# A one-core transformer kernel: unused tiles move its on-chip operands to multiples of 512 bytes

## The chip, the core and the metric

The kernel runs on one core of one Trainium2 chip. Its time is the device time of one execution in microseconds (us), and a kernel is judged by the median of several executions. A separate execution is recorded by the hardware profiler, and every stretch, row and duration below that is not called a median comes from that one recording. Engine names are those of the profile: PE multiplies matrices (PEld is its loading of the operand that stays in the array), DVE and ACT are the vector and the scalar engine, POOL is the general engine, SP issues most transfers (DMA).

## What is computed

Two layers of a diffusion backbone work on 256 latent tokens of width 2048, in float32. Cut to what matters here:

```python
def reference(x, c, ctx, c_ctx, ada_w, ...):
    x_lat, x_ctx = x, ctx
    for l in range(2):
        sh1, sc1, g1, sh2, sc2, g2 = split(silu(c) @ ada_w[l] + ada_b[l], 6)
        h = modulate(x_lat, norm_mix[l], sh1, sc1)
        if l == 0:
            hc = modulate(x_ctx, ...)               # 256 context tokens
            y = even_mixer(h, hc, ...)              # h @ ev_w_in, gated delta rule || attention, @ ev_w_out
        else:
            y = shortconv_mixer(h, ...)             # h @ od_w_in, 3-tap convolution, @ od_w_out
        x_lat = x_lat + g1 * y
        h2 = modulate(x_lat, norm_ffn[l], sh2, sc2)
        x_lat = x_lat + g2 * ((silu(h2 @ w_gate[l]) * (h2 @ w_up[l])) @ w_down[l])
    return rmsnorm(x_lat, final_norm)
```

`ada_w[l]` is 2048 x 12288, `w_gate` and `w_up` are 2048 x 5632, `w_down` is 5632 x 2048. Nearly all bytes and nearly all arithmetic are the weights times a few hundred tokens.

## The kernel before

**Every large product is split into three.** A float32 operand is written as a rounded part (hi) and a remainder (lo), both in the type `float32r`, and a product is hi x hi + hi x lo + lo x hi, three matmuls that add into one PSUM bank. Weights arrive in pieces of 128 rows x 1024 columns (512 KB, tile `raw`). `split_w` (from L236) makes `whi` on ACT (L173) and `wlo` on DVE (L244) from each. The activations are split once per stage, into `hlhi`/`hllo` and `hchi`/`hclo` (normed latent and context tokens of layer 0, L584), `yhi`/`ylo` (the first mixer's output), `fhi`/`flo` (FFN input), `dhi`/`dlo` and `zhi`/`zlo` (the second mixer's input and its gated result), and, for the down projection, `ahi`/`alo`, split piece by piece from `prodT` (L176, L177).

**Two kinds of stream use them.** `tm_stream` holds a 128 x 128 block of the activation in the array and sends 512 columns of `whi` or `wlo` past it: L292, L293 and L295 are its three products, L301, L302 and L303 the same for the last two blocks of a sum. A step of it, one weight piece for two blocks of tokens, is 2 x 2 x 3 = 12 such matmuls. A stream of 2048 rows by 1024 columns has 16 steps, so 192 matmuls; the down projection has 44 steps for each 1024 columns. `fm_stream` does the reverse: a 128 x 128 block of `whi` or `wlo` is held and 256 tokens of h are sent past it (L322). Both load the held block anew for every matmul, so each MATMUL has its LDWEIGHTS.

**What runs when.** First the modulation vectors of layer 0 (L555), then `fm_stream` for keys, values and queries with the delta rule's small products in between, then the attention, then `tm_stream` for ev_w_out (with y), layer 0's FFN (11 streams for gate and up, 88 steps for down), the second mixer (6 streams for od_w_in with d, 2 for od_w_out with z), and layer 1's FFN. Beside these streams the other columns of `ada_w` are read as `araw` and summed on DVE (L376, L411).

**Where tiles lie.** Each tile takes the same byte range in all 128 partitions. Pools are filled from the left or, where `side="right"` is given, from the right end of the on-chip memory, one tile after the other; a pool opened later begins where the earlier one ends. Tiles through the class `Rows` are rounded up to 16 floats, so they begin at multiples of 64 bytes, and nothing in the kernel asks for more. A tile's start therefore depends on the sizes of all tiles before it on its side: `edge` and the tiles of `epool`, `gw` (pool "gdn"), `rpool`, the FFN's `ap_` and the second mixer's `dp` are such predecessors, and the diff touches these.

The order of instructions on each engine comes from the recording layer, which is given the program in the order in which `body` writes it.

Of the kernel before, what the change touches and what calls it, by code (L numbers as in the profile page):

```python
# [23 lines left out]
F32 = mybir.dt.float32  # L24
# [85 lines left out]
def body(tc, x, c, ctx, c_ctx, ada_w, ada_b, norm_mix, norm_ffn, ffn_w_gate, ffn_w_up, ffn_w_down,  # L110
# [27 lines left out]
    def pool(name, bufs=1, stack=root, **kw):  # L138
        if kw.get("space") is not bass.MemoryType.DRAM:
            kw.setdefault("reuse_waits", "tile")  # L140
        p = stack.enter_context(tc.tile_pool(name=name, bufs=bufs, **kw))
        return p if "space" in kw else Rows(p)

    cpool = pool("const")
    edge = pool("edge", side="right").p.tile([128, 8], F32, name="edge")
    epool = pool("even")
    wstk = Stack()
    wp = dict(pool=pool("weights", stack=wstk), raw=RAW, split=3)
# [9 lines left out]
    def smt():  # L158
        small.append(small.pop(0))
        return small[0].tile([128, 512], F32, name="sm", tag="sm")  # L160
# [11 lines left out]
    def acopy(dst, src):  # L172
        ACT.activation(dst, src, AF.Copy)  # L173
# [16 lines left out]
    def transpose(dst, src):  # L190
        n = src.shape[0]
        return PE.transpose(dst, src, ident[:n, :n])  # L192
# [245 lines left out]
    def load_row(l, seg):  # L438
        r = rpool.tile([128, D], F32, name="row", tag="row", bufs=1)
        src = row_d[l, seg]  # L440
        ACT.dma_start(r, bass.AP(tensor=src.tensor, offset=src.offset, ap=[[0, 128], [1, D]]))
        return r
# [36 lines left out]
    def drive(stream, pump=None, n=1, every=1, counts=False):  # L479
        for i, _ in enumerate(stream):  # L480
            steps[0] += counts
            while counts and plan and plan[0][0] <= steps[0]:
                plan.pop(0)[1]()
            if later and i % every == every - 1:
                f, args = later.pop(0)
                f(*args)
            if pump:
                pump(n)
# [262 lines left out]
    gw = pool("gdn", stack=rstk, side="right")  # L751
# [38 lines left out]
    eg = epool.tile([128, 3, 2, 4, 8], F32, name="eg")  # L790
    negegc = epool.tile(gsh, F32, name="negegc")
    brest = epool.tile(gsh, F32, name="brest")

    def gates():
        w = abp
# [370 lines left out]
    lga.close()  # L1166
    yp = pool("y", stack=lgs, side="right")

    yhi, ylo = [], []
    for g in range(3):  # L1170
        for l_, n_, tag in ((yhi, "yhi", "diag"), (ylo, "ylo", "lsol")):
# [85 lines left out]

    rpool = pool("resid")
    xs = rpool.tile([128, 2, D], F32, name="xs")
    ssx = rpool.tile([128, 2, 4], F32, name="ssx")  # L1260
    ss2 = rpool.tile([128, 2], F32, name="ss2")
    jk = rpool.tile([128, 512], F32, name="jk")
# [23 lines left out]
    def norm_h(hi, lo, sc_, sh_):  # L1286


        ns = Stack()
        pool_ = pool("norm", stack=ns)  # L1290
        r = [None, None]
        for n in range(4):
            ks_ = slice(n * 4, n * 4 + 4)
            for t in range(2):
                if not n:
                    r[t] = norm_row(t)
                xt_ = pool_.tile([128, 512], F32, name="xc", tag="xc", bufs=4)
                xi = DVE.tensor_scalar(xt_, xs[:, t, n * 512:(n + 1) * 512], r[t], None, op0=OP.mult)
                p = smt()
                for j in range(4):  # L1300
                    transpose(p[:, j * 128:(j + 1) * 128], xt_[:, j * 128:(j + 1) * 128])
                m = pool_.tile([128, 4, 128], F32, name="modt", tag="modt", bufs=2)
                tok = slice(t * 128, t * 128 + 128)
                for j in range(4):
                    k = n * 4 + j
                    q = p[:, j * 128:(j + 1) * 128]
                    mi = ACT.activation(hi[:, k, tok], q, AF.Identity, bias=sh_[:, k:k + 1], scale=sc_[:, k:k + 1])
                    DVE.tensor_scalar(m[:, j, :], q, sc_[:, k:k + 1], sh_[:, k:k + 1], op0=OP.mult, op1=OP.add)
                DVE.tensor_tensor(lo[:, ks_, tok], m, hi[:, ks_, tok], op=OP.subtract)  # L1309
                if not n:  # L1310
                    behind = (mi if not t else behind[0], xi)
        ns.close()
        return behind

    def split_on_the_fly(pool_, src):
        def f(k):
            hi = pool_.tile([128, 256], F32R, name="ahi", tag="ahi", bufs=3)
            lo = pool_.tile([128, 256], F32R, name="alo", tag="alo", bufs=3)
            s = src(k)
            if len(s.shape) == 3:  # L1320
                split(hi.rearrange("p (t e) -> p t e", t=2), lo.rearrange("p (t e) -> p t e", t=2), s)
            else:
                split(hi, lo, s)
            return lambda t: hi[:, t * 128:(t + 1) * 128], lambda t: lo[:, t * 128:(t + 1) * 128]
        return f
# [32 lines left out]
    def ffn(l, jobs_fn, n_jobs):  # L1358
        fs = Stack()
        hp = pool(f"ffn_h{l}", stack=fs)  # L1360
        hi = hp.tile([128, KT, 256], F32R, name="fhi", tag="fhi", bufs=1)
        lo = hp.tile([128, KT, 256], F32R, name="flo")
        normed = norm_h(hi, lo, scc[l, 3], shc[l, 3])
        ap_ = pool(f"ffn_a{l}", stack=fs)
        jobs = jobs_fn(ap_)
        pump = Pump(jobs, PS[l], n_jobs)
        pp = pool(f"ffn_p{l}", stack=fs)
        prodT = pp.tile([128, FK, 256], F32, name="prodT")

        def lhs(k):  # L1370
            return lambda t: hi[:, k, t * 128:(t + 1) * 128], lambda t: lo[:, k, t * 128:(t + 1) * 128]

        def finish(prod, w, c0):

            for f in range(0, w // 128, 2):
                p = smt()
                for kk in range(2):
                    for t in range(2):
                        transpose(p[:, kk * 256 + t * 128:kk * 256 + (t + 1) * 128],
                                  prod[:, t, (f + kk) * 128:(f + kk + 1) * 128])  # L1380
                acopy(prodT[:, c0 // 128 + f:c0 // 128 + f + 2, :], p.rearrange("p (k t) -> p k t", k=2))

        for c0 in range(0, 5120, 1024):
            sg = pp.tile([128, 2, 1024], F32, name="sg", tag="sg", bufs=1)

            def ge(ti, n, p):
                ACT.activation(sg[:, ti, n * 512:(n + 1) * 512], p, AF.Silu)

            def ue(ti, n, p):
                v = sg[:, ti, n * 512:(n + 1) * 512]  # L1390
                DVE.tensor_tensor(v, p, v, op=OP.mult)

            drive(tm_stream([(ffn_w_gate[l], c0, 1024)], ks, lhs, [0, 1], ge, None if c0 else normed), pump)
            drive(tm_stream([(ffn_w_up[l], c0, 1024)], ks, lhs, [0, 1], ue), pump)
            finish(sg, 1024, c0)
        sg = pp.tile([128, 2, 1024], F32, name="sg", tag="sg", bufs=1)

        def le(ti, n, p):
            v = sg[:, ti, 0:512]
            if n == 0:  # L1400
                ACT.activation(v, p, AF.Silu)
            else:
                DVE.tensor_tensor(v, p, v, op=OP.mult)

        drive(tm_stream([(ffn_w_gate[l], 5120, 512), (ffn_w_up[l], 5120, 512)], ks, lhs, [0, 1], le), pump)
        finish(sg, 512, 5120)
        otf = split_on_the_fly(pp, lambda k: prodT[:, k, :])
        row = load_row(l, 5)
        fn = None
        if l:  # L1410
            fn = hp.tile([128, D], F32, name="fn", tag="fhi", bufs=1)
            ACT.dma_start(fn, bass.AP(tensor=final_norm.tensor, offset=final_norm.offset, ap=[[0, 128], [1, D]]))
        for half in range(2):
            drive(tm_stream([(ffn_w_down[l], half * 1024, 1024)], list(range(FK)), otf, [0, 1],
                            resid_evac(row, half * 1024, fn)), pump)
        pump.finish()
        fs.close()

    ffn(0, lambda ap_: [ada_job(ap_, 0, 5, "row"), ada_job(ap_, 1, 0, "sh"), ada_job(ap_, 1, 1, "sc", gamma=g_mix[1]), ada_job(ap_, 1, 3, "sh"), ada_close()], 132)


    ds = Stack()
    dp = pool("od", stack=ds)
# [1 line left out]
    dlo = dp.tile([128, KT, 256], F32R, name="dlo")  # L1425
    zhi = dp.tile([128, KT, 256], F32R, name="zhi")
    zlo = dp.tile([128, KT, 256], F32R, name="zlo")
    up = [dp.tile([128, 258], F32, name=f"upad{i}") for i in range(2)]
    normed = norm_h(dhi, dlo, scc[1, 0], shc[1, 0])
    adp = pool("od_a", stack=ds)  # L1430
    pump = Pump([ada_job(adp, 1, 2, "row"), ada_job(adp, 1, 4, "sc", gamma=g_ffn[1]), ada_close()], PO, 68)
# [48 lines left out]
    ds.close()  # L1480

    ffn(1, lambda ap_: [ada_job(ap_, 1, 5, "row"), ada_close()], 36)


# [39 lines left out]
```

## Time and profile before

| | |
|---|---|
| median of 3 executions | 2813.17 us (2809.87 to 2813.56) |
| span of the profiled execution | 2817.0 us |
| its share of the full TensorE clock | 0.986 |
| bytes moved | 677.62 MB, 241 GB/s on average |

The record holds no time of the profiled execution other than its span, from the first to the last instruction; it is 3.8 us above the median. The busy time of PE in the profile counts an interval in which any matmul is in flight. Neighbouring matmuls overlap: one of 512 columns takes some 0.39 us from its start to its end, but the next one starts about 0.23 us after it. So PE's real rate is read from the distance between starts, not from the mean duration of a matmul, and a busy share near 100% does not say that the matmuls could not follow one another faster.

### The profile page before, as it was taken

To read this page: it belongs to the slowest core of one execution; us is meant where nothing else is said; L and a number is where in the kernel's file an instruction comes from. 1 tells how busy PE (TensorE), PEld (TensorE's weight loads), DVE (VectorE), ACT (ScalarE), POOL (GpSimd) and SP (SyncE) were. 2 spreads that over 40 slices of the span, in tenths; PEclk is the share of its full clock that TensorE was granted. 3 is DMA by queue.
4 is the path that set the end of the run, shared out by engine and by line. 5 is a ranking of instruction groups with operands and counts; after the bars stand their busy time and mean duration, and the time that the engine had idled before them with its cause. 6 is when DMAs were issued, how large, how long until landed. Compare 5 with 4: busy or idle time off the path is not lost.

```text
span 2817.0 us, 39969 instructions
## 1 busy us (share of the span) xinstructions
PE 2712.2 (96%) x14935; PEld 2260.4 (80%) x14935; DVE 1931.3 (69%) x2653; ACT 1290.4 (46%) x1923; POOL 48.0 (2%) x77
## 2 busy tenths in 40 slices
PE   6999999999989999999999999999999999999998
PEld 3798989887768788888888878787878888888886
DVE  2377877875768888887676667897688644445565
ACT  3267543323454644444455555344454444445554
POOL 0000000000000000000000000000000000000000
PEclk9999999998999999999999999999999999999999
DMA  9944587886658699999775557998659766666563
GB/s 340 328 136 154 150 269 240 289 253 198 194 182 278 215 336 331 347 333 325 271 270 189 189 158 276 325 321 289 197 199 332 239 191 187 187 201 202 189 190 123
DMA packets 284990, 677.62 MB, mean 241 GB/s; under 512 B 57081, under 2 KB 100705, under 8 KB 283387
## 3 DMA queue, kind: packets, MB, share of 16 engines
q1 hardware_dynamic: 280420, 665.59, 71.2%
q10 hardware_dynamic: 4375, 9.48, 0.9%
q8 instruction: 117, 1.92, 0.3%
q14 instruction: 78, 0.64, 0.1%
HBM read 655.54 MB, written 19.43 MB: 240 GB/s over the span
## 4 chain that ended last, share of the span: by engine, by line
PE 67%; DMA 16%; DVE 9%; issue 4%; ACT 3%; SPq 1%; POOL 0%; DVEq 0%; ACTq 0%
PE mm L292 15%; PE mm L293 15%; PE mm L295 15%; DMA araw<-in_ada_w_dram 11%; PE mm L322 9%; DVE acc L376 4%; DVE wlo L244 3%; PE sm L192 2%; PE mm L301 1%; PE mm L303 1%; PE mm L302 1%; DMA bq<-in_ev_rpb_dram 1%; PE sm L555 1%; PE gd L322 1%; DMA acc<-in_ada_b_dram 1%
## 5 line engine op out<-in xcount | busy, mean ns | idle before, releaser
L173 ACT ACTIVATE whi<-raw 128x1024 fp32r<-128x1024 f32 x800 | 842.8, 1059 | 872.2 <-PE mm L295 628.4
L244 DVE TENSOR_TENSOR wlo<-raw,whi 128x1024 fp32r<-128x1024 f32 x800 | 970.2, 1222 | 394.1 <-ACT whi L173 387.0
L293 PE MATMUL mm<-wlo,fhi 128*128 128x512 f32 x1232 | 469.9, 392 | 0.2 <-DVE wlo L244 0.2
L292 PE MATMUL mm<-whi,fhi 128*128 128x512 f32 x1232 | 468.6, 396 | 0.0
L295 PE MATMUL mm<-whi,flo 128*128 128x512 f32 x1232 | 393.4, 392 | 0.1
L376 DVE SCALAR_TENSOR_TENSOR acc<-araw,cT,acc 128x1024 f32<-128x1024 f32 x224 | 287.3, 1283 | 143.4 <-DMA araw<-in_ada_w_dram 131.5
L295 PEld LDWEIGHTS mm<-whi,flo 128*128 128x128 f32 x1232 | 231.1, 188 | 51.1 <-DVE flo L1309 0.3
L293 PEld LDWEIGHTS mm<-wlo,fhi 128*128 128x128 f32 x1232 | 231.6, 188 | 49.4 <-DVE wlo L244 0.6
L292 PEld LDWEIGHTS mm<-whi,fhi 128*128 128x128 f32 x1232 | 232.1, 188 | 48.5
L293 PE MATMUL mm<-wlo,ahi 128*128 128x512 f32 x672 | 258.9, 395 | 0.0
L292 PE MATMUL mm<-whi,ahi 128*128 128x512 f32 x672 | 258.0, 396 | 0.0
L295 PE MATMUL mm<-whi,alo 128*128 128x512 f32 x672 | 210.9, 395 | 0.0
L322 PE MATMUL mm<-hllo,whi 128*128 128x256 f32 x608 | 172.3, 288 | 0.0
L176 ACT ACTIVATE ahi<-prodT 128x256 fp32r<-128x256 f32 x176 | 72.9, 417 | 198.2 <-DVE wlo L244 179.6
L322 PE MATMUL mm<-hlhi,whi 128*128 128x256 f32 x570 | 160.9, 291 | 2.3 <-DVE hlhi L583 1.9
L322 PE MATMUL mm<-hlhi,wlo 128*128 128x256 f32 x570 | 157.8, 288 | 0.5 <-DVE wlo L244 0.5
L411 DVE SCALAR_TENSOR_TENSOR acc<-araw,cT,acc 128x512 f32<-128x512 f32 x192 | 142.7, 747 | 15.5 <-DMA araw<-in_ada_w_dram 13.8
L295 PEld LDWEIGHTS mm<-whi,alo 128*128 128x128 f32 x672 | 126.6, 188 | 29.5
L292 PEld LDWEIGHTS mm<-whi,ahi 128*128 128x128 f32 x672 | 126.6, 188 | 29.4
L293 PEld LDWEIGHTS mm<-wlo,ahi 128*128 128x128 f32 x672 | 126.6, 188 | 29.2
L177 DVE TENSOR_TENSOR alo<-prodT,ahi 128x256 fp32r<-128x256 f32 x176 | 74.4, 424 | 83.9 <-PE mm L295 78.6
L293 PE MATMUL mm<-wlo,dhi 128*128 128x512 f32 x336 | 123.9, 395 | 0.6 <-DVE wlo L244 0.6
(418 smaller groups left out, 4182.1 us busy)
## 6 DMA issues: line engine op xcount, KB each, us to landing
araw<-in_ada_w_dram SPq DMA_DIRECT2D x288, 512.0 KB
raw<-in_ffn_w_down_dram SPq DMA_DIRECT2D x176, 512.0 KB
raw<-in_ffn_w_gate_dram SPq DMA_DIRECT2D x160, 512.0 KB
raw<-in_ffn_w_up_dram SPq DMA_DIRECT2D x160, 512.0 KB
raw<-in_ev_w_in_dram SPq DMA_DIRECT2D x112, 512.0 KB
araw<-in_ada_w_dram SPq DMA_DIRECT2D x192, 256.0 KB
raw<-in_od_w_in_dram SPq DMA_DIRECT2D x96, 512.0 KB
raw<-in_ev_w_out_dram SPq DMA_DIRECT2D x32, 512.0 KB
```

Of the source, the lines that this page charges most:

```text
L173: ACT.activation(dst, src, AF.Copy)
L176: ACT.activation(hi, src, AF.Copy)
L177: (eng or DVE).tensor_tensor(lo, src, hi, op=OP.subtract)
L192: return PE.transpose(dst, src, ident[:n, :n])
L244: last_lo[0] = DVE.tensor_tensor(lo, raw, hi, op=OP.subtract).ins
L292: PE.matmul(ps[ti][n], a, hi[:, n * 512:(n + 1) * 512], start=first, stop=False)
L293: PE.matmul(ps[ti][n], a, lo[:, n * 512:(n + 1) * 512], start=False, stop=False)
L295: last_mm[0] = PE.matmul(ps[ti][n], b, hi[:, n * 512:(n + 1) * 512], start=False, stop=False).ins
L301: PE.matmul(ps[ti][n], lh(t), hi[:, c_], start=False, stop=False)
L322: last_mm[0] = PE.matmul(ps[f][:, n * 256:(n + 1) * 256], wt, mv(w, k), start=False, stop=i == len(ks) - 1 and g == len(group) - 1 and j = ...
L376: DVE.scalar_tensor_tensor(acc, raw, cT[:, k:k + 1], acc, op0=OP.mult, op1=OP.add)
L411: DVE.scalar_tensor_tensor(accs[n], raws.pop(i), cT[:, k:k + 1], accs[n], op0=OP.mult, op1=OP.add)
```

## The change

Six pools get a few bytes that nobody reads or writes, or a tile that is larger than needed, so that the tiles behind them begin elsewhere:

```diff
-    edge = pool("edge", side="right").p.tile([128, 8], F32, name="edge")
+    edge = pool("edge", side="right").p.tile([128, 120], F32, name="edge")
...
     brest = epool.tile(gsh, F32, name="brest")
+    epool.tile([128, 48], F32, name="pad_e")
...
     yp = pool("y", stack=lgs, side="right")
+    gw.tile([128, 48], F32, name="pad_g")
...
     xs = rpool.tile([128, 2, D], F32, name="xs")
+    rpool.tile([128, 80], F32, name="pad_r")
...
         ap_ = pool(f"ffn_a{l}", stack=fs)
+        ap_.tile([128, 80], F32, name="pad_a")
...
-    up = [dp.tile([128, 258], F32, name=f"upad{i}") for i in range(2)]
+    up = [dp.tile([128, 384], F32, name=f"upad{i}")[:, 0:258] for i in range(2)]
```

No instruction is added, removed or moved. On each of the five engines the built program has the same operations on the same tiles in the same order, with waits on the same semaphores, and the PSUM banks are the same. What differs is where tiles begin. The start of each tile in the built program, as the remainder of its byte address divided by 512:

| tiles | before | now |
|---|---|---|
| `raw`, `whi`, `wlo` (weight pieces, all buffers, all stages) | 320 | 0 |
| `h`, `hlhi`, `hllo`, `hchi`, `hclo` | 320 | 0 |
| `yhi`, `ylo` | 128 | 0 |
| `fhi`, `flo` | 0 | 0 |
| `prodT`, `ahi`, `alo`, `sg` | 192 | 0 |
| `dhi`, `dlo`, `zhi`, `zlo` | 0 | 0 |
| `u_t`, `b_t`, `ocv` | 128 | 0 |
| `acc`, `araw` in layer 0's first mixer | 448 | 0 |
| `acc`, `araw` in the FFN | 0 | 320 |
| `acc`, `araw` in the second mixer | 128 | 0 |
| tiles of the delta rule (`kT`, `ktok`, `gm`, `state`, `xdT` and others) | 128 | 0 |
| `araw0` and `xn` of the start | 128 and 0 | 192 and 64 |

The blocks that a matmul holds are 512 bytes wide in a partition and those that it sends are 1024 or 2048, so each such block has the remainder of its tile.

## The prediction

> **What bounds the kernel now.** I read the page's busy times first, then PE's busy time stage by stage, then the chain of waits inside single stages for the distance between matmul starts.
>
> ```profile
> PE 2712.2 (96%) x14935; PEld 2260.4 (80%) x14935; DVE 1931.3 (69%) x2653; ACT 1290.4 (46%) x1923; POOL 48.0 (2%) x77
> ```
>
> The next view cuts the last two thirds of the span into stages: layer 0's FFN (gate and up, then down), the second mixer (its input product, then its output product), layer 1's FFN.
>
> ```profile
> core 0: us, PE busy (x), PEclk, DMA share, GB/s
> 944.00:1425.00 481.00, 479.67 (x2163) 1.00 0.90 320
> 1425.00:1680.00 255.00, 250.55 (x1102) 0.99 0.61 197
> 1680.00:1955.00 275.00, 270.57 (x1216) 0.99 0.87 300
> 1955.00:2074.00 119.00, 114.26 (x523) 0.97 0.55 177
> 2074.00:2557.00 483.00, 482.28 (x2163) 1.00 0.70 225
> 2557.00:2817.00 260.00, 246.35 (x1065) 0.98 0.54 174
> sum 1873.00, PE 1843.68; mean PE 307.28
> ```
>
> In 1873 us PE is without work for 29. DMA is high in two of the stages and yet PE does not stand still there. So these stages are worth their number of matmuls times the distance between two starts, and that distance is what this change can touch, since no instruction moves.
>
> The distance is not the same everywhere, although the matmuls of lines L292, L293 and L295 are all 512 columns wide. Rows of the chain, in order of time (start, length, what; "x2" are two matmuls): first layer 1's FFN, then its like for the second mixer's output product, the first mixer's output product, layer 0's down projection, and the latent-and-context product with h.
>
> ```profile
> 2310.35 0.46 PE mm L295 x2
> ...
> 2325.46 0.46 PE mm L295 x2
> ```
>
> ```profile
> 2020.87 0.46 PE mm L295 x2
> ...
> 2029.11 0.46 PE mm L295 x2
> ```
>
> ```profile
> 852.93 0.47 PE mm L295 x2
> ...
> 864.13 0.47 PE mm L295 x2
> ```
>
> ```profile
> 1491.03 0.47 PE mm L295 x2
> ...
> 1527.29 0.46 PE mm L295 x2
> ```
>
> ```profile
> 514.88 0.23 PE mm L293
> ...
> 526.67 0.23 PE mm L295
> ```
>
> A pair at L295 returns after six matmuls. FFN: 11 returns, 15.11 us / 66 = **228.9 ns**. z: 6 returns, 8.24 / 36 = **228.9**. y: 8 returns, 11.20 / 48 = **233.3**. Down: 26 returns, 36.26 / 156 = **232.4**. With h: 52 matmuls one by one, 11.79 / 52 = **226.7**. All sent pieces (`whi`, `wlo`) begin at remainder 320 of 512. Only the held operand's remainder differs, and the distance goes with it: 320 gives 226.7; 0 gives 228.9 (fhi, and zhi the same); 192 gives 232.4; 128 gives 233.3. The shortest is where both begin at the same remainder. That dhi, also at 0, has 228.9 as well is taken over from these.
>
> **The change part by part.** It puts held and sent operand of all these products at remainder 0, so equal, as they are today only with h. My theory is that the difference of the two remainders decides, not the remainders: the load of the next block runs beside the matmul, and where the two begin alike it costs least. Then every row above goes to 226.7 ns. The counts, from the loops and checked on two rows of groups:
>
> ```profile
> L292 PE MATMUL mm<-whi,fhi 128*128 128x512 f32 x1232 | 468.6, 396 | 0.0
> L292 PE MATMUL mm<-whi,ahi 128*128 128x512 f32 x672 | 258.0, 396 | 0.0
> ```
>
> Gate and up: 11 streams x 192 x 2 layers = 4224 (a third at L292 and L301 is 1408, of which 14 of 16 steps, 1232, are at L292, as the row says). Down: 88 steps x 12 x 2 = 2112 (704 a third, 42 of 44 steps 672). Second mixer: 6 x 192 = 1152 with d, 2 x 192 = 384 with z. First mixer's output: 2 x 192 = 384 with y. The sum:
>
> - gate and up, 4224 x (228.9 - 226.7) = 9.3 us
> - d and z, 1536 x 2.2 = 3.4 us
> - down, 2112 x (232.4 - 226.7) = 12.0 us
> - y, 384 x (233.3 - 226.7) = 2.5 us
>
> Together **27 us**. Of the 576 wide products with h (384 for the attention's values, 192 for the output gate) nothing changes by this theory: they are at equal remainders before and after. Their 256-wide form at L322 holds a block of the weights and sends h:
>
> ```profile
> 339.93 23.03 PE mm L322 x192
> ```
>
> 23.03 / 192 = 119.9 ns, 320 against 320; I cost it at nothing. Ahead of 944 us only y has a term.
>
> The other engines read and write the same tiles. DVE's sum over `araw` stands at remainder 0 in layer 0's FFN and at 128 in the second mixer; the groups of DVE in 1000 to 1200 us and in 1750 to 1900 us:
>
> ```profile
> L376 DVE SCALAR_TENSOR_TENSOR acc<-araw,cT,acc 128x1024 f32<-128x1024 f32 x55 | 70.6, 1283 | 33.2 <-DMA araw<-in_ada_w_dram 32.2 <-issue 0.3
> L376 DVE SCALAR_TENSOR_TENSOR acc<-araw,cT,acc 128x1024 f32<-128x1024 f32 x39 | 50.0, 1282 | 24.5 <-DMA araw<-in_ada_w_dram 24.3
> ```
>
> 1283 against 1282 ns: DVE does not see the remainder. Nor do the transfers, as far as these rows go: the wait for `araw` is 32.2 / 55 = 0.59 us each at remainder 0 and 24.3 / 39 = 0.62 at 128. So the one place where the change makes a start less round (`araw` and `acc` in the FFN, 0 to 320) I cost at nothing. Were it the whole difference of those two waits, 0.03 us x 160 sums in both FFNs = 5 us of DVE, hidden by PE's own work, since DVE is 69% busy and the splits have spare time; were that cover gone, 5 us. The start's `araw0` and `xn` shift by 64 bytes likewise.
>
> What is late next when PE goes 1 to 2.5% faster in these stages? A step of 12 matmuls falls from 2.75 to 2.72 us.
>
> ```profile
> L244 DVE TENSOR_TENSOR wlo<-raw,whi 128x1024 fp32r<-128x1024 f32 x800 | 970.2, 1222 | 394.1 <-ACT whi L173 387.0
> ```
>
> DVE needs for it 1.22 us of split and at most one sum of 1.28. There is room, and the 90% DMA share of the first FFN stage comes from `araw` pieces that are fetched ahead.
>
> The trace cannot show what a sent piece at remainder 0 costs, since in before all of them start at 320. Bounds: from above, the slowest row, 233.3 ns for everything: 5760 x 4.4 + 2112 x 0.9 + 576 x 6.6 = 31 us lost. From below, the same products while the clock is at half:
>
> ```profile
> 636.00:640.00 4.00, 4.00 (x10) 0.50 0.87 282
> ```
> ```profile
> 636.53 0.43 PE mm L293
> ...
> 639.94 0.43 PE mm L292
> ```
>
> 8 matmuls in 3.41 us are 426 ns, at full clock 213: at half speed nothing is added to the 512 columns. At 213 for everything the gain would be 5760 x 15.9 + 2112 x 19.4 + 384 x 20.3 + 576 x 13.7 = 148 us, and some 3000 at L322 (3 x 768 + 2 x 384 by the loops) x 13 = 39 more. I take 226.7, the nearest row with equal remainders, between those ends.
>
> [...]
>
> **The rivals.**
>
> *A larger gain.* A piece that begins at a round address may by itself be sent faster. For it: blocks of 32 and 64 columns instead of 128 are held at L777 and L778, with the same h at 320 sent past:
>
> ```profile
> 183.50 0.28 PE L780 MATMUL sm<-hllo,abw 128*32 128x256 f32 x1
> ...
> 186.79 0.28 PE L777 MATMUL sm<-hllo,abw 128*32 128x256 f32 x1
> ```
>
> 29 distances in 3.29 us, 113.4 ns against 119.9, so 6.5 ns of the excess over 106.5 (half of 213) belong to the wide load and another 6.9 to something else, perhaps the start at 320. Against it: these 113.4 have the sent operand at 320 too, so the start alone cannot be all of it. If half of the wide load's part went (223.3 instead of 226.7), the gain would be 5760 x 5.6 + 2112 x 9.1 + 384 x 10 + 576 x 3.4 = 57 us, with 3000 x 3.3 = 10 at L322 67: **2746 us**. If all of it went, 220: 106 us, **2707**.
>
> *No difference, or little.* The distance may go with the held operand alone, whatever is sent: then 0 is 228.9 for all, down gains 2112 x 3.5 = 7.4, y 1.7, and h loses 576 x 2.2 = 1.3: -8 us, **2805**. Or it goes with something that comes with these stages and not with the address: **2813**. For it: each remainder appears in one or two kinds of stage only, so address and stage cannot be told apart in all rows; against it, that fhi and zhi agree across two different stages. That the padding misses its target cannot be: the addresses are in the build.
>
> *Slower.* Remainder 0 for both may be a bad pair: the held block's load and the sent piece then start at the same place at the same time, and if the place and not the difference counts, the meeting may cost what it costs with y. Priced at the upper end above, 31 us: **2844 us**. It decides once the new distance is over the present mean of the 8832 wide matmuls, (5760 x 228.9 + 2112 x 232.4 + 384 x 233.3 + 576 x 226.7) / 8832 = 229.8. Against it: the pair at 320 and 320 is the best row.
>
> **How the numbers follow.** 2817.0 - 27 = 2790 for a profiled span; the span stands 3.8 over the median, so 2813.2 - 27 = **2786 us** for the median. Its own range is 2778 to 2794 (the spread of 4 us among the executions, and a quarter of the sum). Chances: forecast 0.52, larger gain 0.18, none or little 0.19 (0.13 of it within 0.2%, which is about what a measurement of this kernel can tell from no change), slower 0.11. A range for 8 in 10 takes in the small cases, up to 2819, and half of the larger gain, down to 2746; outside are the slower case and the other half, 0.2. Faster is 0.52 + 0.18 + 0.06 = 0.76, same 0.13, slower 0.11.
>
> **What would show it.** In the profile of the changed kernel the pairs at L295 should return every 1.360 us in all four stages, not 1.373 (FFN, z), 1.394 (down) or 1.400 (y), and L322 stay at 119.9. If FFN and down agree with each other at another value, the theory of equal remainders is right and the size wrong. If down falls and the FFN stays, the held operand alone counts. If L322 falls, the sent operand counts for itself. What would make the forecast wrong beside this: a wait of DVE for `araw` in the FFN that grows beyond 0.62 us each and reaches PE.

## The result and the profile after

| | before | after |
|---|---|---|
| median of the executions taken together | 2812.49 us (2809.87 to 2813.56, 4) | 2791.36 us (2787.81 to 2799.25, 4) |
| profiled execution | | 2799.25 us |
| its span | 2817.0 us | 2797.5 us |
| its share of the full TensorE clock | 0.986 | 0.987 |

The ratio after / before is 0.9933, with a 95% interval from 0.9914 to 0.9952: faster by 21 us. Two later comparisons of the same two kernels gave 0.9905 [0.9884, 0.9927] and 0.9918 [0.9900, 0.9936], 27 and 22 us.

The page's busy times after, to be laid beside those of before:

```profile
PE 2688.9 (96%) x14935; PEld 2258.6 (81%) x14935; DVE 1930.2 (69%) x2653; ACT 1291.2 (46%) x1923; POOL 47.9 (2%) x77
```

PE's time changed by 23.3 us, that of DVE, ACT and the weight loads by 2 us at most, and the counts not at all. The stages of after, cut where those of before were (the bounds are shifted so that each stretch holds as many matmuls, to within one; the columns are start and end, length, PE's busy time and matmuls, clock, DMA share, rate):

```profile
core 0: us, PE busy (x), PEclk, DMA share, GB/s
944.58:1423.11 478.53, 475.79 (x2162) 1.00 0.90 321
1423.11:1672.55 249.44, 244.77 (x1101) 0.99 0.63 203
1672.55:1943.43 270.88, 266.29 (x1216) 1.00 0.87 306
1943.43:2061.27 117.84, 113.40 (x524) 0.97 0.56 176
2061.27:2543.67 482.40, 479.69 (x2162) 1.00 0.70 226
2543.67:2797.50 253.83, 240.23 (x1064) 0.98 0.55 179
```

The two down projections (second and last row) lost 5.6 and 6.2 us, the second mixer 4.1 and 1.2. The two gate-and-up stages lost 2.5 and only 0.6. That last figure is the one that does not fit, and it is taken up below.

Rows of the chain of waits of after: layer 1's FFN, the second mixer's output product, the first mixer's output product, and the down projection of layer 0; in each pair of rows the first and the last of an unbroken series. Then 192 matmuls at L322.

```profile
2300.48 0.45 PE mm L295 x2
...
2314.08 0.45 PE mm L295 x2
...
2008.26 0.45 PE mm L295 x2
...
2016.42 0.45 PE mm L295 x2
...
893.56 0.45 PE mm L295 x2
...
899.00 0.45 PE mm L295 x2
...
1479.80 0.45 PE mm L295 x2
...
1515.16 0.45 PE mm L295 x2
...
340.77 23.04 PE mm L322 x192
```

10 returns in 13.60 us, 6 in 8.16, 4 in 5.44 and 26 in 35.36: **1.360 us per return in all four, 226.7 ns per matmul**. L322 is at 23.04 / 192 = 120.0 ns, as before.

### The profile page after: what moved, and what is told of

Same layout as the page of the kernel before. It is cut to its first block, busy times and chain, and to the rows that moved or that the text cites. A ratio compares the mean times of both kernels' runs of the same rounds, so it can differ in the third digit from the quotient of the medians.

```text
span 2797.5 us, 39969 instructions
## 1 busy us (share of the span) xinstructions
PE 2688.9 (96%) x14935; PEld 2258.6 (81%) x14935; DVE 1930.2 (69%) x2653; ACT 1291.2 (46%) x1923; POOL 47.9 (2%) x77
## 4 chain that ended last, share of the span: by engine, by line
PE 74%; DMA 12%; DVE 7%; ACT 3%; issue 2%; SPq 1%; POOL 0%; DVEq 0%; ACTq 0%
PE mm L292 17%; PE mm L293 17%; PE mm L295 17%; PE mm L322 10%; DMA araw<-in_ada_w_dram 8%; DVE acc L376 2%; DVE wlo L244 2%; PE sm L192 2%; PE mm L301 2%; PE mm L303 2%; PE mm L302 2%; DMA bq<-in_ev_rpb_dram 1%; PE sm L555 1%; PE gd L322 1%; ACT whi L173 1%
## 5 line engine op out<-in xcount | busy, mean ns | idle before, releaser
L292 PE MATMUL mm<-whi,fhi 128*128 128x512 f32 x1232 | 467.0, 395 | 0.0
L295 PE MATMUL mm<-whi,flo 128*128 128x512 f32 x1232 | 391.1, 390 | 0.1
L376 DVE SCALAR_TENSOR_TENSOR acc<-araw,cT,acc 128x1024 f32<-128x1024 f32 x224 | 287.2, 1282 | 144.2 <-DMA araw<-in_ada_w_dram 134.1
L295 PEld LDWEIGHTS mm<-whi,flo 128*128 128x128 f32 x1232 | 231.3, 188 | 48.8 <-DVE flo L1312 0.3
L292 PEld LDWEIGHTS mm<-whi,fhi 128*128 128x128 f32 x1232 | 232.4, 189 | 47.0
L292 PE MATMUL mm<-whi,ahi 128*128 128x512 f32 x672 | 254.4, 390 | 0.0
L295 PE MATMUL mm<-whi,alo 128*128 128x512 f32 x672 | 207.2, 389 | 0.0
L322 PE MATMUL mm<-hllo,whi 128*128 128x256 f32 x608 | 171.6, 287 | 0.0
L322 PE MATMUL mm<-hlhi,whi 128*128 128x256 f32 x570 | 159.6, 288 | 2.3 <-DVE hlhi L583 1.8
L322 PE MATMUL mm<-hlhi,wlo 128*128 128x256 f32 x570 | 157.1, 287 | 0.5 <-DVE wlo L244 0.5
L295 PEld LDWEIGHTS mm<-whi,alo 128*128 128x128 f32 x672 | 126.2, 188 | 26.2
L292 PEld LDWEIGHTS mm<-whi,ahi 128*128 128x128 f32 x672 | 126.2, 188 | 26.1
```

The source lines that it names most:

```text
L292: PE.matmul(ps[ti][n], a, hi[:, n * 512:(n + 1) * 512], start=first, stop=False)
L295: last_mm[0] = PE.matmul(ps[ti][n], b, hi[:, n * 512:(n + 1) * 512], start=False, stop=False).ins
L322: last_mm[0] = PE.matmul(ps[f][:, n * 256:(n + 1) * 256], wt, mv(w, k), start=False, stop=i == len(ks) - 1 and g == len(group) - 1 and j = ...
L376: DVE.scalar_tensor_tensor(acc, raw, cT[:, k:k + 1], acc, op0=OP.mult, op1=OP.add)
```

## The experiments

In the edits below the lines are changes to the changed kernel. "Difference" is the remainder at which the held block begins minus that at which the sent piece begins.

**1. The changed kernel again**, with no edit, to tell what the first recording lost by chance.

> The changed kernel once more, for a second recording and a closer ratio. Theory (equal remainders): the pairs at L295 return every 1.360 us again, and the median is 19 to 27 us under the one of before. The first recording lost some 8 us of the 27 in layer 0's and layer 1's gate and up stages, where PE waited 2.9 us at 91 us into layer 1's FFN and 1.9 us at 220 us into layer 0's. If these waits belong to the kernel (DVE's fixed order meets a PE that comes earlier) they stand at the same places here; if they are chance, they stand elsewhere or are absent and the stages are 3 us shorter.

Measured: 2785.05 us (2780.04 to 2791.19) against 2811.74, ratio 0.9905 [0.9884, 0.9927]; its profiled span is 2783.0. Two recordings of one program differ by 14.5 us. Where: most of it lies ahead of y, in a stretch in which the sum has no term. Its row in the first recording of after, then in the second (start and end, length, PE busy, clock):

```profile
45.20:788.90 743.70, 708.21 (x5974) 0.98 0.71 226
```

```profile
45.60:778.20 732.60, 701.14 (x5972) 0.99 0.72 230
```

11.1 us, with less of PE's time at half clock in the second (its clock records add up to 20.5 us there, 34.1 in the first; 37.5 in before). Another 3.5 us lie in layer 1's FFN. PE's transposes at L192 waited there once for DVE, some 92 us into the stage: at 2137 us in the first recording and at 2126 us in the second. The waits of 2134 to 2142 us in the first and of 2122 to 2130 us in the second (who waited, for what: us in total, times, longest):

```profile
PE sm L192 <- DVE sg L1395: 2.5, 1, 2.5
```

```profile
PE sm L192 <- DVE sg L1395: 1.2, 1, 1.2
```

In both, DVE had a transpose, a split and a reduction to do before `sg`. So the wait stands at the same place, as the expectation says of a wait that belongs to the kernel, but its length varies: it is 0.6 us in before, 0.2 in experiment 2, 2.4 in experiment 3 and under 0.1 in experiment 8. The other wait, for a weight piece 220 us into layer 0's stage (1.5 us in the first recording), is absent in the second. Layer 1's stage takes 478.90 instead of 482.40; besides the shorter wait, PE was at half clock there for none of it instead of 3.4 us.

**2. `araw` and `acc` of the FFN back at remainder 0**, everything else as in the changed kernel:

```diff
-        ap_.tile([128, 80], F32, name="pad_a")
...
+        pp.tile([128, 80], F32, name="pad_p")
```

> The changed kernel with the FFN's unused tile placed behind the accumulator and its raw tiles instead of ahead of them: acc and araw of the FFN are at remainder 0 as in before, all matmul operands at 0 as after. If araw at remainder 320 is what gave part of the gain back, this is 3 to 8 us faster than the changed kernel and the late waits of PE in the gate and up stages fall to 7 and 5 us; if the remainder of araw does not matter, it is within 3 us of it. Matmul distances 226.7 ns in both cases.

Measured: 2786.71 us (2781.77 to 2789.78), 0.9914 [0.9893, 0.9935], inside the interval of experiment 1. DVE's group over `araw` in 1000 to 1200 us, after (at 320) and here (at 0):

```profile
L376 DVE SCALAR_TENSOR_TENSOR acc<-araw,cT,acc 128x1024 f32<-128x1024 f32 x55 | 70.5, 1282 | 35.0 <-DMA araw<-in_ada_w_dram 34.0 <-issue 0.3
```

```profile
L376 DVE SCALAR_TENSOR_TENSOR acc<-araw,cT,acc 128x1024 f32<-128x1024 f32 x54 | 69.2, 1282 | 32.9 <-DMA araw<-in_ada_w_dram 31.8 <-issue 0.9
```

1282 ns each in both, and 34.0 / 55 = 0.62 us of waiting against 31.8 / 54 = 0.59. The two medians of four executions differ by 1.7 us, so these runs show no worth of the remainder of `araw`. PE's waits in layer 0's gate and up did not fall either: 4.8 us, against 3.2 in the first recording.

**3. Every operand at remainder 320** in place of 0:

```diff
-    edge = pool("edge", side="right").p.tile([128, 120], F32, name="edge")
+    edge = pool("edge", side="right").p.tile([128, 40], F32, name="edge")
...
-    epool.tile([128, 48], F32, name="pad_e")
```

> Every matmul operand of the named tiles at remainder 320, none at 0: weights and h where before had them, y, FFN, down and second-mixer operands moved to 320. If equal remainders decide: 226.7 ns in all stages and the time of the changed kernel, about 2790. If multiples of 512 count for themselves: 228 to 233 ns in gate and up, down, y and z, and a time of 2800 to 2830. If the h stage was short for a reason of its own: FFN and down keep 228.9 and 232.4, about 2812.

Measured: 2794.28 us (2785.36 to 2794.55), 0.9929 [0.9908, 0.9951]. The chain in layer 0's down projection and in layer 1's FFN:

```profile
1474.72 0.45 PE mm L295 x2
...
1533.20 0.45 PE mm L295 x2
...
2320.46 0.47 PE mm L295 x2
...
2354.48 0.45 PE mm L295 x2
```

43 returns in 58.48 us and 25 in 34.02: 226.7 and 226.8 ns. So a multiple of 512 has no merit of its own: **equal starts at 320 do the same as equal starts at 0**. The median is 9 us above that of experiment 1. The two intervals overlap, and the distances leave no room for a difference of this kind; where the 9 us come from, if they are real, is not shown.

**4. A different difference in every stage**, the weights staying at 0. This takes the address and the stage apart, which the prediction could not do.

```diff
-    edge = pool("edge", side="right").p.tile([128, 120], F32, name="edge")
+    edge = pool("edge", side="right").p.tile([128, 200], F32, name="edge")
...
+        hp.tile([128, (16, 112)[l]], F32, name="pad_h")
...
-        ap_.tile([128, 80], F32, name="pad_a")
+        ap_.tile([128, (96, 176)[l]], F32, name="pad_a")
...
+    dp.tile([128, 64], F32, name="pad_d")
...
+    dp.tile([128, 32], F32, name="pad_z")
```

> The changed kernel with the sent weight pieces at 0 and the held operand at another remainder in each stage: layer 0 gate and up 64, layer 0 down 128, first mixer output (y) 192, second mixer input (d) 256, layer 1 down 320, second mixer output (z) 384, layer 1 gate and up 448. If the difference held minus sent decides, the three differences of before come back in other stages: y (192) 228.9 ns, z (384) 232.4, layer 1 down (320) 233.3; the other four are new and lie between 226.7 and 233.3. If the held operand's own remainder decides: y 192 gives 232.4, layer 0 down 128 gives 233.3, layer 1 down 320 gives 226.7. If neither, all keep 226.7. Time by the first theory 2800 to 2825.

Measured: 2818.17 us (2814.94 to 2822.05), ratio to before 1.0025 [1.0011, 1.0040]. The chain in the second mixer's input product (difference 256) and in layer 1's down projection (320):

```profile
1933.17 0.45 PE mm L295 x2
...
1949.49 0.47 PE mm L295 x2
...
2614.52 0.47 PE mm L295 x2
...
2673.32 0.47 PE mm L295 x2
```

12 returns in 16.32 us are 226.7 ns; 42 in 58.80 are 233.3. The chain that ended last doesn't run through the earlier stages in this recording, so here PE's timeline (start, time until the last of them ends), for the first FFN (64), its down projection (128) and the first mixer's output product (192):

```profile
1311.01 0.63 PE L295 MATMUL mm<-whi,flo 128*128 128x512 f32 x2
...
1320.81 0.63 PE L295 MATMUL mm<-whi,flo 128*128 128x512 f32 x2
...
1502.42 0.64 PE L295 MATMUL mm<-whi,alo 128*128 128x512 f32 x2
...
1512.18 0.64 PE L295 MATMUL mm<-whi,alo 128*128 128x512 f32 x2
...
850.63 0.62 PE L295 MATMUL mm<-whi,ylo 128*128 128x512 f32 x2
...
858.87 0.62 PE L295 MATMUL mm<-whi,ylo 128*128 128x512 f32 x2
```

7 returns in 9.80 us, 7 in 9.76 and 6 in 8.24: 233.3, 232.4 and 228.9 ns. Read in the same way, z (384) has 232.4 and layer 1's FFN (448) 228.9.

| difference modulo 256 | here, in the stage | before, in the stage |
|---|---|---|
| 0 | 226.7: d | 226.7: h |
| 64 | 233.3: gate and up of layer 0; down of layer 1 | 233.3: y (128 - 320) |
| 128 | 232.4: down of layer 0; z | 232.4: down (192 - 320) |
| 192 | 228.9: y; gate and up of layer 1 | 228.9: gate and up, z (0 - 320) |

Each value of before comes back at the same difference in another stage, and with other addresses. **The difference sets the distance, with a period of 256 bytes**; neither the stage, nor the held operand's own remainder, nor that of the sent piece does. By the table and the loops' counts this kernel should stand over the changed one by 2112 x 6.7 + 2112 x 2.2 (gate and up) + 1056 x 5.7 + 1056 x 6.7 (down) + 384 x 2.2 (y) + 384 x 5.7 (z), which is 35 us; by the medians it is 33.

**5. Finer differences**: in the two FFNs 32 and 224, in the two down projections 96 and 160, in the second mixer 16 (d) and 240 (z), and h at 64 (latent) and 128 (context), with the weights at 0.

```diff
+    hlp.tile([128, 16], F32, name="pad_hl")
+    hcp.tile([128, 16], F32, name="pad_hc")
...
+        hp.p.tile([128, (8, 56)[l]], F32, name="pad_h")
...
-        ap_.tile([128, 80], F32, name="pad_a")
+        ap_.p.tile([128, (96, 64)[l]], F32, name="pad_a")
...
+    def off(name, n):
+        t = dp.tile([128, KT * 256 + 64], F32R, name=name)[:, n:n + KT * 256]
+        return t.rearrange("p (k t) -> p k t", k=KT)
+
+    dhi, dlo, zhi, zlo = off("dhi", 4), off("dlo", 4), off("zhi", 60), off("zlo", 60)
```

> Steps finer than 64 bytes, weight pieces at 0, the held operand minus them at: layer 0 gate and up 32, layer 0 down 96, layer 1 down 160, layer 1 gate and up 224, second mixer input (d) 16, its output (z) 240. The map with 64-byte steps gave, modulo 256: 0 226.7 ns, 64 233.3, 128 232.4, 192 228.9. If the cost runs smoothly with the difference: 16 and 32 between 226.7 and 233.3, 96 near 233, 160 near 230.6, 224 and 240 between 228.9 and 226.7, and nothing below 226.7, so the changed kernel has the best there is. If whole units of 64 bytes count: 16 and 32 like 0 or like 64, 224 and 240 like 192 or like 0. If there is a better place: one of them below 226.7. Also the latent tokens h at 64 and the context tokens at 128, sent past weights at 0 (differences 192 and 128): L322 at 122 to 126 ns if its matmuls pay as the wide ones do, 119.9 if they don't.

Measured: 2822.32 us (2815.91 to 2827.37), ratio to before 1.0046 [1.0018, 1.0074]. The chain in the first down projection (96), z (240), and the FFN of layer 1 (224), then a row at L322 with the weights held and h sent:

```profile
1473.82 0.47 PE mm L295 x2
...
1531.45 0.47 PE mm L295 x2
...
1974.87 0.45 PE mm L295 x2
...
1993.91 0.45 PE mm L295 x2
...
2423.64 0.47 PE mm L295 x2
...
2458.64 0.47 PE mm L295 x2
...
337.30 22.56 PE mm L322 x192
```

41 returns in 57.63 us are 234.3 ns, the longest of all; 14 in 19.04 are 226.7; 25 in 35.00 are 233.3. The mean over the long series of each stage is 233.3 at 32 and at 160. At 16, in the second mixer's input product, there are two values. Two series from PE's timeline:

```profile
1700.95 0.63 PE L295 MATMUL mm<-whi,dlo 128*128 128x512 f32 x2
...
1759.75 0.63 PE L295 MATMUL mm<-whi,dlo 128*128 128x512 f32 x2
...
1788.84 0.62 PE L295 MATMUL mm<-whi,dlo 128*128 128x512 f32 x2
...
1806.52 0.62 PE L295 MATMUL mm<-whi,dlo 128*128 128x512 f32 x2
```

42 returns in 58.80 us are 233.3 ns, 13 in 17.68 are 226.7, at the same addresses. About three quarters of the matmuls in the unbroken series of this stage are at the first value. The distance changes where a longer gap between two matmuls (over 245 ns) breaks the series, never inside one; at 16, then, the difference alone does not settle it. So 240 is as good as 0, 16 only in part, 224 not, and **no difference is below 226.7**. L322 surprised: at unequal starts it fell to 22.56 / 192 = 117.5 ns.

**6. Half of the held block.** As experiment 4, but outside the first matmul of a sum and its last two blocks only 64 of the 128 columns of the held block are loaded; half of the output rows then lack most of their sum.

```diff
-                            PE.matmul(ps[ti][n], a, lo[:, n * 512:(n + 1) * 512], start=False, stop=False)
+                            PE.matmul(ps[ti][n][0:64], a[:, 0:64], lo[:, n * 512:(n + 1) * 512], start=False, stop=False)
```

(the lines of the other two products likewise)

> The kernel of the map, but the streams that hold activations load and use only 64 of the 128 columns of each held block, except in the first matmul of a sum and in its last two blocks (so half of the output rows lack most of their sum). If the load that runs beside the sent piece is what costs, a load of half the width meets it for half as long: all stages fall to about 220 ns (213.3 + the 6.9 that the narrow blocks at L777 show), whatever their remainder. If the remainders act in another way than through the load, the distances of the map stay: 233.3 in layer 0 gate and up, 228.9 in layer 1 gate and up, 232.4 and 233.3 in down.

Measured: 2808.86 us in a single execution. The chain in the second mixer (256) and layer 1's down projection (320); the shifted line L296 is L295 of the others:

```profile
1923.87 0.46 PE mm L296 x2
...
1939.05 0.45 PE mm L296 x2
...
2602.59 0.46 PE mm L296 x2
...
2661.22 0.47 PE mm L296 x2
```

11 returns in 15.18 us are 230.0 ns (226.7 with the whole block), 42 in 58.63 are 232.7 (233.3). Neither of the two things expected came. Nor is a load of half the columns half as long: before's profile has 134 ns for 64 columns (L778) and 188 for 128 (L292). Half a load neither takes away nor halves the excess over 213 ns, and at equal starts it makes the distance longer. At the unequal differences it is shorter by 0.5 to 2.6 ns (means over the unbroken series: 228.4 instead of 228.9 in layer 1's gate and up, 231.2 instead of 232.4 in layer 0's down, 229.8 instead of 232.4 in z), and at 64 there are two values, 231.1 and about 232.7, of which the second pair of rows shows the longer. A plain account, in which the time of the load or its bytes are what the matmul pays for, does not hold. The edit halves the output rows too, so the load was not changed alone.

**7 and 8. h at 240, and the changed kernel beside it.** The wide products that hold h have the difference 240 then; at L322, where the weights are held and h is sent, it is 16.

```diff
-    h0 = hlp.tile([128, 512], F32R, name="h0")
-    hs_hi = (hlp.tile([128, KT - 1, 256], F32R, name="hlhi"), hcp.tile([128, KT - 1, 256], F32R, name="hchi"))
-    hs_lo = (hlp.tile([128, KT, 256], F32R, name="hllo"), hcp.tile([128, KT, 256], F32R, name="hclo"))
+    hl = hlp.p.tile([128, 60 + 512 + (2 * KT - 1) * 256], F32R, name="hl")[:, 60:]
+    hc = hcp.p.tile([128, 60 + (2 * KT - 1) * 256], F32R, name="hc")[:, 60:]
...
+    h0 = hl[:, 0:512]
+    hs_hi = (blocks(hl, 512, KT - 1), blocks(hc, 0, KT - 1))
+    hs_lo = (blocks(hl, 512 + (KT - 1) * 256, KT), blocks(hc, (KT - 1) * 256, KT))
```

> The changed kernel with h at remainder 240 (weights at 0): the wide products that hold a block of h have a difference of 240, at which 512-wide products took 226.67 ns in an earlier run, and the 256-wide products that hold a block of the weights have a difference of 16. Theory (wide products: 0 and 240 are alike; 256-wide ones are a little faster at unequal starts, 117.5 to 117.8 at 192 and 128 instead of 120.0): L322 falls to about 117.6, the wide products with h stay at 226.7, and some 3000 x 2.4 = 7 us go, about 2779 where the changed kernel reads 2786. Rival 1 (only some differences are better for the 256-wide form; 16 is not one of them): L322 stays at 120.0 and the time is that of the changed kernel. Rival 2 (the 256-wide form at 16 is hit as the 512-wide form is, 232.25 instead of 226.67, so by 2.5%): L322 at 122.8 and 8 us more, 2794. One thing beside it: the parts of h lie in one tile for each stream; should its waits differ, that shows as late starts in the first layer alone.

> The changed kernel as it is, beside the run with h at 240 on one chip: 2786 us, within 6, L322 at 120.0 and the pairs at L295 every 1.360 us. It is there to compare times only.

Measured: 2783.29 us (2777.70 to 2791.18), 0.9897 [0.9877, 0.9917], beside 2789.23 us (2783.48 to 2792.31), 0.9918 [0.9900, 0.9936]. PE's timeline with h at 240, the first and the last of 33 matmuls in a row:

```profile
329.77 0.28 PE L322 MATMUL mm<-hc,whi 128*128 128x256 f32 x1
...
333.52 0.28 PE L322 MATMUL mm<-hc,wlo 128*128 128x256 f32 x1
```

3.75 us / 32 = 117.2 ns where the changed kernel has 120.0, and the wide products with h stay at 226.7. The distance at L322 is thus shown; the gain in time, 6 us by the medians where some 3000 x 2.8 = 8 were to be had, is not, as the two intervals overlap.

## Why the prediction was right

**The mechanism.** Its theory was that the difference of the two starts decides and not the starts, and that every row goes to 226.7 ns. All four stages did (result), equal starts at another address did the same (experiment 3), and the old distances follow the difference into other stages (experiment 4). It spoke of remainders of 512; the runs show a period of 256 (226.7 ns at differences 0 and 256, 233.3 at 64 and 320, 232.4 at 128 and 384, 228.9 at 192 and 448). The reason that it gave, a load that costs least where the two begin alike, is not shown: with half of each block loaded the distance rose from 226.7 to 230.0 ns at difference 256 (experiment 6).

**L322** was costed at nothing and stayed at 120.0. **`araw` at 320** was costed at nothing, with a bound of 5 us on DVE: the waits of 0.62 and 0.59 us happen to be the two values that the bound was made from, and the time did not follow (experiment 2).

**The size.** The prices per matmul were right to 0.1 ns; the sum of 27 us arrived as 21, 27 and 22. The stages' lengths (first matmul of one to first matmul of the next, in the trace) show where the rest is. Five recordings have equal starts in all these stages: the three of the changed kernel and experiments 2 and 3.

| stage | in the sum | mean of the five, less before |
|---|---|---|
| y | -2.5 | -1.7 |
| gate and up, layer 0 | -4.6 | -0.9 |
| down, layer 0 | -6.0 | -5.3 |
| second mixer, d | -2.5 | -3.6 |
| z | -0.8 | -0.8 |
| gate and up, layer 1 | -4.6 | -3.6 |
| down, layer 1 | -6.0 | -6.1 |
| together | -27 | -22 |

So about 5 us are given back, most of them in layer 0's gate and up. PE's waits in this stage, before and in experiment 8:

```profile
PE sm L192 <- DVE sg L1391: 1.3, 3, 0.8
PE sm L192 <- DVE modt L1308: 0.4, 1, 0.4
```

```profile
PE sm L192 <- DVE sg L1395: 3.2, 2, 2.6
PE mm L293 <- DVE wlo L244: 0.5, 1, 0.5
PE sm L192 <- DVE modt L1311: 0.2, 1, 0.2
```

PE waited 1.7 us for DVE before and 3.9 here; the first recording of after has 3.2, experiments 1, 2 and 3 have 1.5, 4.8 and 4.5. Waits for `wlo`, a weight piece not yet split, are absent before and present in four of the five. The step that was too simple is "What is late next": it compared DVE's work for a mean step, 1.22 + 1.28 us, with 2.72 us, and took that for room enough, while DVE comes late where a transpose and a reduction of the modulation sums fall between (experiment 1). The longer waits make 1.9 us of the 3.7 on average. The same stage has 1.1 us at half clock in before and 2.2 to 7.0 in the five, 3.7 on average; as a matmul takes some 426 ns there instead of 226.7, this is worth another 1.2 us, an estimate from these numbers. The rest is not traced. This is one recording of before against five, so the direction is shown better than the size.

Ahead of y, before's recording and the first of after are as long as each other (742.9 and 743.7 us) while the other four are 6 to 13 us shorter, with less time at half clock; none of the change's terms lies there, so a difference of two spans can be luck of that kind. The medians of experiment 1 do not show it: the executions of both kernels have the same granted clock there (0.986 to 0.991). But experiments 2 and 3, with equal starts too and beside the same executions of before, stand 25 and 17 us under it, so that the 27 which matches the sum is the upper end of a spread, and the 22 of the table fits the five comparisons (17 to 27) better.

**The rivals.** The larger gain fell: the sent piece at a round address is not faster by itself (experiment 3), and no difference goes below 226.7. "With the held operand alone" fell: fhi stayed at 0 and its products went from 228.9 to 226.7 as the weights moved. "The stage" fell with experiment 4. "A bad pair" fell: 0 with 0 is as good as 320 with 320. Bad pairs there are, but they are unequal ones: experiments 4 and 5 are 33 and 37 us above experiment 1 (experiment 5 ran on another chip), and 0.25 and 0.46% above before.

**What stays open** is what the difference acts through. The trace's own stamps show that the distances are not one number but a short cycle (ns between successive starts):

```
equal          227 226 227 227 226 227
64 (y)         231 236 231 236
192 (FFN)      226 229 232 226 229 232
128 (down)     228 230 233 241 232 231 232
```

The unequal ones have cycles of two, three and seven matmuls. What makes them, and the two values at difference 16, which change only where a series is broken (experiment 5), no run here shows.

## What to carry to other kernels

Where 512-column float32r matmuls load a new block each and PE is the bound, start the held and the sent operand at equal byte addresses modulo 256: that took 226.7 ns per matmul here. The unequal ones run here took 228.9 to 234.3, so 1 to 3% of these stages, but for 240 (226.7) and 16 (226.7 and 233.3). Where the two start together did not matter: 0 and 320 gave the same distance, 226.7. Read the rate from the distance between starts, stage by stage: a PE that is 96% busy hid this entirely. A gain of 1% on the bounding engine can bring waits on the next one into view (some 2 us of 27 here), so expect a part of it back.

## What the runs showed of the hardware

- The distance depends on held minus sent start with a period of 256 bytes: 226.7 ns at 0 and 240, 228.9 at 192, 232.4 at 128, 233.3 at 32, 64, 160 and 224, 234.3 at 96, all for 512 columns of float32r. The neighbours of 0 are not alike: 240 costs nothing, while at 16 the same matmuls stand at 233.3 ns for most of the stage and at 226.7 in between (experiment 5).
- At equal starts the distance at full clock is over half of that at half clock by the same amount for both widths: 226.7 - 213.3 = 13.3 ns for 512 columns, 120.0 - 106.7 = 13.3 for 256. Before has 426 to 427 and 213 to 214 ns at half clock; the means over before and after are 426.6 and 213.5, in proportion to the columns, and 213.3 and 106.7 are their halves.
- For 256 columns the sign turns at the differences run: 117.5 ns with h at 64 and 128 (experiment 5) and 117.2 at difference 16 (experiment 7) against 120.0 at equal starts.
- A held block of half the columns, with half the output rows, costs more at equal starts (230.0 instead of 226.7 ns at difference 256) and 0.5 to 2.6 ns less at unequal ones (experiment 6).
- Two recordings of one program on one core differ by 14.5 us in span (experiment 1). 11.1 of them lie in the first 790 us, where PE stood at half clock for 34.1 us in one and 20.5 in the other; by the two distances above this is worth some 6 us, an estimate.
